# A hybrid decoder step on one core: products and weight splits moved from GpSimd to VectorE and ScalarE

## The chip, the cores and the metric

The kernel runs on one core of a Trainium2 chip. The core has a matrix engine (TensorE, PE in the profile), a vector engine (VectorE, DVE), a scalar engine (ScalarE, ACT), a general engine (GpSimd, POOL) and DMA queues, here all issued from SyncE (SP). Each engine executes its instructions in the order in which they stand in its own queue and waits on semaphores. The metric is the device time of one execution in microseconds (us), smaller being better.

## The reference

One layer of a recurrent decoder is applied to a prompt of 512 tokens and to 8 single-token samples with the same weights, all in float32. What is computed, cut to its core:

```python
xm, ig, fg, og, zm, rcols, zr, u, zs, gm = split(layer_norm(x) @ w_in)     # 1024 -> 12424 columns
# A: mLSTM: conv4, q k v, chunked exponential gating -> hm ; y_m = (hm * silu(zm)) @ w_bm
# B: RWKV-7: per token  S <- S diag(w) + (S(-kk))(kk*a)^T + v k^T ; y = S r ; y_r = (... * silu(zr)) @ w_br
# C: S5, 64 groups of 16 channels, 64 complex states each:
lb = exp(lam * dt);  bb = (lb - 1) / lam * b
s_t = lb * s_{t-1} + bb u_t ;  ys = gelu(Re(c s_t) + d u_t)
ys = ys * sigmoid(ys @ s_glu_w + s_glu_b) ;  y_s = (ys * silu(zs)) @ w_bs
x = layer_norm(ALPHA * x + (sum_b sigmoid(g_b) * y_b) @ w_out)
```

The outputs are x for prompt and samples and the new states of the three mixers.

## The kernel before

**Matrix products.** The 520 token columns stand along the free axis in two halves (256 and 264). A weight block of 1024 x 128 is loaded in two raw tiles (`load_w`, line 121, three buffers `wraw`), and each is split into a rounded high part `whi` on ScalarE (line 130) and the rest `wlo = wraw - whi` (line 131) on the engine that the list `weng` names. `gemm` then runs three products (high-high, high-low, low-high) over eight row blocks for each half and hands the PSUM tile to an evacuation on VectorE or ScalarE. `weng` is GpSimd up to the end of the RWKV stage (138 half splits) and VectorE after it (120).

**Stages.** After the entry normalisation come set-up work (the gates of the mLSTM, the S5 constants in `s5_setup`), the RWKV stage (about 100 to 745 us), the S5 stage with branch B's projections woven in (`interleave`, about 745 to 1005 us), the mLSTM stage with the S5 branch's projections woven in, and the last branch with the output product. During the RWKV stage a list of spare projections (`fills`) gives TensorE work between the recurrence's own small products.

**RWKV.** Eight channel blocks are prepared two at a time. `elementwise` builds the rows `bk` (beta rows, then scaled by the chunk's decay `pc`, and transposed to `bkt`) and `ar`. For each pair `inverse` inverts triangular blocks on VectorE: one transpose `lu`, then 31 steps of a product `itmp` and an addition `xi` (lines 589 and 591). `chain` then walks through eight chunks.

**S5.** Four passes (`pi`), each of 16 groups in two halves. A pass loads `uu` and `br` from DRAM, forms `bb` (line 959 on), then `eb` and `gm` (for each a product by `pf`'s real part on VectorE, one by its imaginary part on GpSimd, `et` and `gt`, and an addition on VectorE), and from them the kernels `ko` and, by TensorE, the drives `bu`. The phasors `ph` (64 powers of a unit complex number for 8 columns) are grown by doubling: 6 steps of 6 instructions on GpSimd, each on what the step before made. VectorE multiplies `bu` by `ph` (`ta`, `tb`, lines 1041 and 1042), scans (`z`), multiplies back (`ta` on VectorE, `tb` on GpSimd, line 1053) and writes the states `ss`, which TensorE turns into `ys`. `ph`, `bb`, `uu` have one buffer each, so that a pass's phasors begin when the pass before has last read them.

**Order.** A scheduler in the build fixes each engine's order ahead of time, so a change of engine for one instruction moves others too. Line numbers are those of the kernel before.

Of the kernel before, what the change touches and what calls it, by code (L numbers as in the profile page):

```python
# [39 lines left out]
def hybrid_step(ctx: ExitStack, tc: tile.TileContext, I, O):  # L40
    nc = tc.nc
    V, A, G, TE = nc.vector, nc.scalar, nc.gpsimd, nc.tensor
# [76 lines left out]
    weng = [G, G]  # L119
# [272 lines left out]
def rwkv(tc, I, O, env):  # L392
    e = type("E", (), env)
    nc = tc.nc
    V, A, G, TE = nc.vector, nc.scalar, nc.gpsimd, nc.tensor
# [4 lines left out]
    e.weng[:] = [G, G]  # L400
# [79 lines left out]
    def elementwise(ct, st):  # L480
        ci = ct % 2
# [28 lines left out]
        G.tensor_copy(bk[:, :, 2 * CH:3 * CH], bk[:, :, 0:CH])  # L510
# [391 lines left out]


def s5(tc, I, O, env):
# [20 lines left out]
    for pi in range(KT // 2):  # L925
# [33 lines left out]
        G.tensor_tensor(bb[:, 0], br[:, 0], cb(cr), op=ALU.mult)  # L959
        G.tensor_tensor(bt[:, 0], br[:, 1], cb(cis), op=ALU.mult)  # L960
        G.tensor_tensor(bb[:, 1], br[:, 1], cb(crs), op=ALU.mult)
        G.tensor_tensor(bt[:, 1], br[:, 0], cb(nci), op=ALU.mult)
# [11 lines left out]
        for j in range(2):  # L974
# [728 lines left out]
```

## Time and profile before

| what | value |
|---|---|
| time, median of 3 runs | 1435.56 us (1435.4 to 1437.0) |
| profiled execution, its own time | 1430.04 us |
| its span, first to last instruction | 1428.2 us |
| TensorE busy | 1291.1 us (90%) |
| VectorE busy | 952.2 us (67%) |
| ScalarE busy | 618.3 us (43%) |
| GpSimd busy | 568.4 us (40%) |
| mean granted TensorE clock | 0.954 |

Durations below come from the profiled execution. Its time is its span and 1.8 us around it, and lies 5.5 us under the median of the runs. Shares of busy time are means over stages whose limits differ, so the rows below are cut by stage.

### The profile page before, as it was taken

Reading aid. Unit: us, or ns where it says so; the run is one execution under the profiler, and the core shown is the slowest. Engines: PE = TensorE matmul, PEld = TensorE weight load, DVE = VectorE, ACT = ScalarE, POOL = GpSimd, SP = SyncE. Lnnn points to the kernel's source line nnn. Section 1 sums busy time; section 2 is a strip of 40 time slices with the busy share of each in tenths; the row PEclk is TensorE's granted clock in tenths of the full one; section 3 lists DMA queues with packets and bytes.
Section 4 is the critical chain, followed back from the end, with each engine's and each line's share of the span. In section 5 each row is a group of like instructions: output and inputs, shape, how many; then the busy total and the mean of one; then the engine's idle time right before and its main releaser. Section 6 shows DMA issues by size and latency. Waiting matters only on the chain.

```text
span 1428.2 us, 27605 instructions
## 1 busy us (share of the span) xinstructions
PE 1291.1 (90%) x10509; PEld 1162.1 (81%) x10509; DVE 952.2 (67%) x1950; ACT 618.3 (43%) x1322; POOL 568.4 (40%) x723
## 2 busy tenths in 40 slices
PE   5889989998999899998996888897899999999897
PEld 4888888877987788997976788787888798799765
DVE  6784693469336843789535997577775784665857
ACT  4446537354735463241232332232765775443230
POOL 3445544444444454447406775872000012103710
PEclk9999999999998999998998899997899999999999
DMA  5342222212221222344427453434767676466241
GB/s 181 84 117 81 80 74 63 75 42 68 66 71 42 79 64 75 96 129 149 122 69 131 105 104 91 102 77 117 225 198 255 212 224 207 149 197 194 82 118 60
DMA packets 244275, 166.92 MB, mean 117 GB/s; under 512 B 54424, under 2 KB 219674, under 8 KB 243870
## 3 DMA queue, kind: packets, MB, share of 16 engines
q1 hardware_dynamic: 244142, 165.15, 41.3%
q8 instruction: 83, 1.36, 0.4%
q14 instruction: 50, 0.41, 0.1%
HBM read 124.13 MB, written 38.68 MB: 114 GB/s over the span
## 4 chain that ended last, share of the span: by engine, by line
PE 52%; DVE 22%; POOL 8%; DMA 8%; issue 6%; ACT 3%; SPq 1%; DVEq 0%; ACTq 0%; POOLq 0%
PE g L62 33%; PE cy L62 3%; DVE xi L591 3%; DVE itmp L589 3%; PE cr L62 2%; PE gg L62 2%; POOL ph L954 1%; DVE wlo L131 1%; POOL pht L952 1%; POOL pht L953 1%; PE qk L62 1%; PE nd L62 1%; POOL et L981 1%; PE s L62 1%; PE lw L62 1%
## 5 line engine op out<-in xcount | busy, mean ns | idle before, releaser
L62 PE MATMUL g<-xh,whi 128*128 128x264 f32 (+1 forms) x1552 | 463.3, 299 | 40.2 <-DVE th L1500 15.0
L62 PE MATMUL g<-xl,whi 128*128 128x264 f32 (+1 forms) x1552 | 458.0, 295 | 1.0 <-POOL xl L217 0.5
L62 PE MATMUL g<-xh,wlo 128*128 128x264 f32 (+1 forms) x1552 | 457.2, 295 | 0.0
L62 PEld LDWEIGHTS g<-xh,whi 128*128 128x128 f32 x1552 | 303.6, 196 | 52.3 <-DVE th L1500 16.4
L62 PEld LDWEIGHTS g<-xl,whi 128*128 128x128 f32 x1552 | 303.9, 196 | 6.2 <-POOL xl L217 0.8
L62 PEld LDWEIGHTS g<-xh,wlo 128*128 128x128 f32 x1552 | 303.5, 196 | 4.9 <-issue 0.8
L130 ACT ACTIVATE whi<-wraw 128x512 fp32r<-128x512 f32 x258 | 151.6, 625 | 222.0 <-PE g L62 152.1
L131 POOL TENSOR_TENSOR wlo<-wraw,whi 128x512 fp32r<-128x512 f32 x138 | 192.7, 1416 | 134.7 <-ACT whi L130 122.6
L131 DVE TENSOR_TENSOR wlo<-wraw,whi 128x512 fp32r<-128x512 f32 x120 | 111.6, 956 | 29.5 <-ACT whi L130 27.4
L591 DVE TENSOR_TENSOR xi<-xi,itmp 128x31 f32<-128x31 f32 (+15 forms) x124 | 56.6, 456 | 3.2
L589 DVE TENSOR_TENSOR itmp<-lu,xi 128x31 f32<-128x31 f32 (+15 forms) x124 | 53.9, 435 | 3.0
L555 DVE TENSOR_TENSOR lr<-gg,maskg 64x256 f32<-64x256 f32 x32 | 13.5, 422 | 59.9 <-ACT la L554 59.8
L650 DVE SCALAR_TENSOR_TENSOR xv<-xv,pc,cy 64x64 f32<-64x64 f32 x112 | 31.2, 279 | 29.5 <-PE cy L62 24.9
L637 POOL COPY xv<-yv 64x128 f32<-64x128 f32 x64 | 24.8, 389 | 58.6 <-PE cy L62 48.2
L1547 POOL TENSOR_TENSOR mg<-mg,gth 128x256 f32<-128x256 f32 (+1 forms) x24 | 18.4, 782 | 72.6 <-DVE gth L1546 59.5
L62 PE MATMUL g<-ysh,whi 128*128 128x256 f32 (+1 forms) x128 | 38.3, 311 | 7.9 <-ACT ysh L258 5.6
L62 PE MATMUL g<-w_bmh,wlo 128*128 128x264 f32 (+1 forms) x128 | 37.5, 294 | 7.5 <-DVE wlo L131 7.4
L1547 POOL TENSOR_TENSOR mg<-mg,gt 128x256 f32<-128x256 f32 (+1 forms) x16 | 16.1, 1011 | 67.3 <-DVE gt L1546 67.3
L298 DVE COPY zf<-g 128x256 f32<-128x256 f32 (+1 forms) x56 | 23.8, 424 | 28.7 <-PE g L62 28.3
L644 DVE COPY yv<-cr 64x128 f32<-64x128 f32 x32 | 9.0, 281 | 50.2 <-PE cr L62 43.8
L1279 POOL COPY cvo<-xm 128x11 f32<-128x11 f32 x8 | 4.6, 572 | 91.9 <-ACT xm L1277 70.8
L645 ACT COPY yv<-cr 64x128 f32<-64x128 f32 x32 | 8.4, 262 | 75.6 <-DVE yv L644 75.4
(574 smaller groups left out, 3257.2 us busy)
## 6 DMA issues: line engine op xcount, KB each, us to landing
wraw<-in_w_in_dram SPq DMA_DIRECT2D x194, 256.0 KB
zsave<-zf SPq DMA_DIRECT2D x36, 260.0 KB
cn<-in_state_mlstm_c_dram SPq DMA_DIRECT2D x32, 256.0 KB
out_dram<-cn SPq DMA_DIRECT2D x32, 256.0 KB
yb<-yssave SPq DMA_DIRECT2D x16, 260.0 KB
zz<-zsave SPq DMA_DIRECT2D x16, 260.0 KB
wraw<-in_w_br_dram SPq DMA_DIRECT2D x16, 256.0 KB
wraw<-in_s_glu_w_dram SPq DMA_DIRECT2D x16, 256.0 KB
```

What stands on the lines that cost most here:

```text
L62: TE.matmul(out, lhsT, rhs, start=start, stop=stop)
L130: A.activation(hi[:, k, 0:m], raw[:, :, 0:m], AF.Copy)
L131: eng.tensor_tensor(lo[:, k, 0:m], raw[:, :, 0:m], hi[:, k, 0:m].bitcast(F32), op=ALU.subtract)
L298: V.tensor_copy(z[:, s:s + n], p)
L589: V.tensor_tensor(tv, lu[:, s + 1:32, s:s + 1].to_broadcast([P, r, w]), xi[:, s:s + 1, 0:w].to_broadcast([P, r, w]), op=ALU.mult)
L591: V.tensor_tensor(xi[:, s + 1:32, 0:w], xi[:, s + 1:32, 0:w], tv, op=ALU.add)
L637: G.tensor_copy(xv[hs(1 - pi), pi], yv[hs(1 - pi), pi, :, n, :])
L650: V.scalar_tensor_tensor(dst, xv[hs(pi), pi, ci, :], pcs[ci][hs(pi), n:n + 1], psn[hs(pi), ci, :], op0=ALU.mult, op1=ALU.add)
L952: G.tensor_tensor(tg[0], b(0), ph[:, q, :, 0:n], op=ALU.mult)
L953: G.tensor_tensor(tg[1], b(1), ph[:, 1 - q, :, 0:n], op=ALU.mult)
L954: G.tensor_tensor(ph[:, q, :, n:2 * n], tg[0], tg[1], op=ALU.add if q else ALU.subtract)
L1547: G.tensor_tensor(dst, dst, g, op=ALU.add)
```

## The change

Work is taken from GpSimd and given to VectorE and ScalarE:

- all weight splits run on VectorE (`weng` is VectorE throughout);
- the scaling of `bk` by `pc`, one GpSimd instruction of 128x1536, becomes eight ScalarE instructions of 128x192; a copy of 128x512 moves to ScalarE too;
- in S5 the products `bb`, `bt`, `et`, `gt` and `tb` run on VectorE;
- the 64 phasors are no longer grown by doubling in each pass. The set-up builds two small tables (powers 1 to 8, and multiples of 8), 40 small instructions, and writes them to DRAM in four DMAs; a pass loads its table (one DMA) and forms all 64 products with three VectorE instructions of 128x512 for each of the real and imaginary parts.

```diff
-    weng = [G, G]
+    weng = [V, V]
...
-    e.weng[:] = [G, G]
...
-        G.tensor_copy(bk[:, :, 2 * CH:3 * CH], bk[:, :, 0:CH])
+        A.activation(bk[:, :, 2 * CH:3 * CH], bk[:, :, 0:CH], AF.Copy)
...
-        G.tensor_tensor(bk, bk, st["pc"][ci].unsqueeze(2).to_broadcast([P, NCH, 3 * CH]), op=ALU.mult)
+        for n in range(NCH):
+            A.activation(bk[:, n], bk[:, n], AF.Copy, scale=st["pc"][ci][:, n:n + 1])
...
+        tb = sy.tile([P, 4, 2, 2, 8, 8], F32, name="tb")
...
+        def grow(k, by, i0, n):
+            tgs = [sy.tile([P, 4, 8, 4], F32, tag="tbt", bufs=2, name="tbt")[:, :, :, 0:n] for _ in range(2)]
+            b = lambda q: pw8(by[0], q, by[1], by[1] + 1).to_broadcast([P, 4, 8, n])
+            o = by[1] + 1
+            for q in range(2):
+                for j in range(2):
+                    V.tensor_tensor(tgs[j], b(j), pw8(k, q ^ j, i0, i0 + n), op=ALU.mult)
+                V.tensor_tensor(pw8(k, q, o, o + n), tgs[0], tgs[1], op=ALU.add if q else ALU.subtract)
...
+        for n in (1, 2, 4):
+            grow(1, (1, n - 1), 0, n)
...
+        for n in (1, 2, 4):
+            grow(0, (0, n), 1, min(n, 3))
+        for a in range(KT // 2):
+            dma(e.phsave[a], tb[:, a].rearrange("p k q c n -> p (k q c n)"))
...
-        G.tensor_copy(ph[:, :, :, 0], pr[:, 1:3, 8 * pi:8 * pi + 8])
-        n = 1
-        while n < SN:
-            b = lambda q: ph[:, q, :, n - 1:n].to_broadcast([P, 8, n])
-            for q in range(2):
-                tg = [sp.tile([P, 8, 32], F32, tag="pht", bufs=2, name="pht")[:, :, 0:n] for _ in range(2)]
-                G.tensor_tensor(tg[0], b(0), ph[:, q, :, 0:n], op=ALU.mult)
-                G.tensor_tensor(tg[1], b(1), ph[:, 1 - q, :, 0:n], op=ALU.mult)
-                G.tensor_tensor(ph[:, q, :, n:2 * n], tg[0], tg[1], op=ALU.add if q else ALU.subtract)
-            n *= 2
+        tb = sp.tile([P, 2, 2, 8, 8], F32, tag="pht", bufs=1, name="tb")
+        dma(tb.rearrange("p k q c n -> p (k q c n)"), e.phsave[pi])
+        for q in range(2):
+            tg = sp.tile([P, 8, SN], F32, tag="pg", bufs=1, name="pg")
...
+            V.tensor_tensor(v4(ph[:, q]), hi_(0), lo_(q), op=ALU.mult)
+            V.tensor_tensor(v4(tg), hi_(1), lo_(1 - q), op=ALU.mult)
+            V.tensor_tensor(ph[:, q], ph[:, q], tg, op=ALU.add if q else ALU.subtract)
...
-        G.tensor_tensor(bb, bb, bt, op=ALU.add)
+        V.tensor_tensor(bb, bb, bt, op=ALU.add)
...
-            G.tensor_tensor(et, pw(pf, 1, 0), bx(1), op=ALU.mult)
+            V.tensor_tensor(et, pw(pf, 1, 0), bx(1), op=ALU.mult)
...
-            G.tensor_tensor(gt, pw(pf, 1, 1), cx(1), op=ALU.mult)
+            V.tensor_tensor(gt, pw(pf, 1, 1), cx(1), op=ALU.mult)
...
-                G.tensor_tensor(tb, zz[1], si if q == 0 else co, op=ALU.mult)
+                V.tensor_tensor(tb, zz[1], si if q == 0 else co, op=ALU.mult)
```

What the scheduler made of it is shown at two places. The first is VectorE's queue at the first block inverse of the RWKV stage, which before holds only the inverse's own steps at its beginning:

```order
L555 TENSOR_TENSOR lr<-gg,maskg 64x256 x3
L579 STREAM_TRANSPOSE lu<-la 128x1024
L589 TENSOR_TENSOR itmp<-lu,xi 128x31
L591 TENSOR_TENSOR xi<-xi,itmp 128x31
L589 TENSOR_TENSOR itmp<-lu,xi 128x60
L591 TENSOR_TENSOR xi<-xi,itmp 128x30x2
L589 TENSOR_TENSOR itmp<-lu,xi 128x87
```

After the change the same place reads (`wlo` are weight splits of later projections; line numbers are one higher):

```order
L580 STREAM_TRANSPOSE lu<-la 128x1024
L590 TENSOR_TENSOR itmp<-lu,xi 128x31
L592 TENSOR_TENSOR xi<-xi,itmp 128x31
L590 TENSOR_TENSOR itmp<-lu,xi 128x60
L592 TENSOR_TENSOR xi<-xi,itmp 128x30x2
L590 TENSOR_TENSOR itmp<-lu,xi 128x87
L592 TENSOR_TENSOR xi<-xi,itmp 128x29x3
L131 TENSOR_TENSOR wlo<-wraw,whi 128x512
L590 TENSOR_TENSOR itmp<-lu,xi 128x112
L131 TENSOR_TENSOR wlo<-wraw,whi 128x512
L592 TENSOR_TENSOR xi<-xi,itmp 128x28x4
```

Two half splits have moved in between the inverse's steps; over the whole inverse there are 12, and 8, 8 and 12 in the other three.

The second place is GpSimd's queue in the third S5 pass before, where the phasor steps (`pht`, `ph`) and the products stand behind one another:

```order
L987 TENSOR_TENSOR gt<-pk,ca 128x1024
L981 TENSOR_TENSOR et<-pk,bb 128x1024
L954 TENSOR_TENSOR ph<-pht 128x8x4
L1048 COPY ss<-pk 128x8x8
L1049 MEMSET ss 128x8
L987 TENSOR_TENSOR gt<-pk,ca 128x1024
L959 TENSOR_TENSOR bb<-br,pk 128x256
L961 TENSOR_TENSOR bb<-br,pk 128x256
L952 TENSOR_TENSOR pht<-ph 128x8x4
L953 TENSOR_TENSOR pht<-ph 128x8x4
L963 TENSOR_TENSOR bb<-bb,bt 128x512
L954 TENSOR_TENSOR ph<-pht 128x8x4
```

After the change GpSimd holds none of these, and VectorE's queue reads, from the last states `ss` of the second pass on:

```order
L1081 TENSOR_TENSOR ss<-ta,tb 64x4x64 x4
L978 TENSOR_TENSOR ph<-tb 128x512 x2
L996 COPY ca<-ccp 128x512
L980 TENSOR_TENSOR ph<-ph,pg 128x512
L131 TENSOR_TENSOR wlo<-wraw,whi 128x512
L990 TENSOR_SCALAR cc<-cc 128x2x64
L1010 TENSOR_TENSOR gm<-pk,ca 128x1024
L1012 TENSOR_TENSOR gt<-pk,ca 128x1024
L1006 TENSOR_TENSOR et<-pk,bb 128x1024
L131 TENSOR_TENSOR wlo<-wraw,whi 128x512
L989 TENSOR_SCALAR cc<-cc 128x2x64
L979 TENSOR_TENSOR pg<-tb 128x512
```

The phasors (lines 978 to 980), `gt` and `et` (1012, 1006) now stand in VectorE's queue among its own products `gm`, `eb` and the weight splits of the branch woven in.

## Rows read from the trace of the kernel before

**Rows 1.** The page: busy us of each engine (share of the span) xinstructions.
```profile
PE 1291.1 (90%) x10509; PEld 1162.1 (81%) x10509; DVE 952.2 (67%) x1950; ACT 618.3 (43%) x1322; POOL 568.4 (40%) x723
```

**Rows 2.** Windows: three stretches; us, each engine busy (xinstructions), granted clock, DMA share, GB/s.
```profile
30.00:105.00 75.00, 64.43 (x502) 61.79 (x500) 58.99 (x154) 32.79 (x65) 33.56 (x53) 0.93 0.36 92
105.00:745.00 640.00, 606.41 (x5401) 543.73 (x5400) 389.01 (x753) 283.01 (x641) 295.62 (x354) 0.96 0.29 81
745.00:1005.00 260.00, 209.51 (x1737) 197.95 (x1736) 192.81 (x321) 81.02 (x166) 161.02 (x232) 0.90 0.48 106
```

**Rows 3.** Chain of waits from 745 to 1005 us: shares by line; one piece.
```profile
by line: issue 13.5%; POOL ph L954 8.1%; POOL pht L952 8.0%; POOL pht L953 7.7%; POOL et L981 6.7%; PE g L62 6.6%; POOL gt L987 5.5%; DVE ss L1056 3.6%; DVE z L1044 3.1%; DVE wlo L131 2.5%; DMA uu<-ud 2.4%; DMA br<-in_s_b_im_dram 2.2%; DVE 
...
760.51 5.66 DMA br<-in_s_b_im_dram
```

**Rows 4.** Timeline of GpSimd in the third S5 pass: start us, us, what.
```profile
887.95 0.35 POOL L952 TENSOR_TENSOR pht<-ph 128x8 f32<-128x8 f32 x1
...
893.84 2.05 POOL L987 TENSOR_TENSOR gt<-pk,ca 128x1024 f32<-128x1024 f32 x1
895.84 2.05 POOL L981 TENSOR_TENSOR et<-pk,bb 128x1024 f32<-128x1024 f32 x1
...
921.80 0.74 POOL L954 TENSOR_TENSOR ph<-pht 128x256 f32<-128x256 f32 x1
```

**Rows 5.** Timeline of VectorE at the same place; idle before in brackets.
```profile
920.46 0.42 DVE L1041 TENSOR_TENSOR ta<-bu,ph 128x256 f32<-128x256 f32 x1 [5.72 <-POOL ph L954]
922.57 0.42 DVE L1042 TENSOR_TENSOR tb<-bu,ph 128x256 f32<-128x256 f32 x1 [1.68 <-POOL ph L954]
```

**Rows 6.** VectorE by form, 745 to 1005 us: busy us, mean ns, idle before.
```profile
L131 DVE TENSOR_TENSOR wlo<-wraw,whi 128x512 fp32r<-128x512 f32 x42 | 35.5, 863 | 6.0 <-ACT whi L130 5.9
L988 DVE TENSOR_TENSOR gm<-gm,gt 128x1024 f32<-128x1024 f32 x8 | 16.0, 2003 | 9.4 <-POOL gt L987 9.4
...
L1594 DVE SCALAR_TENSOR_TENSOR yb<-yb,par,th 128x520 f32<-128x520 f32 x8 | 12.1, 1526 | 1.4 <-DMA yb<-ybsave 1.4
...
L1041 DVE TENSOR_TENSOR ta<-bu,ph 128x256 f32<-128x256 f32 x16 | 6.5, 408 | 16.5 <-POOL ph L954 16.4
```

**Rows 7.** Timeline, two collisions: VectorE and GpSimd each on 128x1024 products.
```profile
806.05 2.04 POOL L981 TENSOR_TENSOR et<-pk,bb 128x1024 f32<-128x1024 f32 x1
806.09 3.08 DVE L980 TENSOR_TENSOR eb<-pk,bb 128x1024 f32<-128x1024 f32 x1
...
852.32 1.24 DVE L980 TENSOR_TENSOR eb<-pk,bb 128x1024 f32<-128x1024 f32 x1
...
852.45 3.01 POOL L981 TENSOR_TENSOR et<-pk,bb 128x1024 f32<-128x1024 f32 x1
```

**Rows 8.** Line 131, the weight split: duration ns min/median/max on each engine.
```profile
L131 POOL TENSOR_TENSOR wlo<-wraw,whi x138: 1257/1290/2273, 12.3 to 707.3; 128x512 fp32r<-128x512 f32 x138
L131 DVE TENSOR_TENSOR wlo<-wraw,whi x120: 671/687/8165, 715.8 to 1352.0; 128x512 fp32r<-128x512 f32 x120
```

**Rows 9.** Windows: the four block inverses; the first and the sum.
```profile
162.70:215.10 52.40, 45.64 (x339) 43.50 (x338) 48.90 (x91) 23.17 (x48) 23.41 (x27) 0.93 0.24 66
...
sum 207.70, PE 184.23 PEld 165.44 DVE 191.89 ACT 91.27 POOL 87.03; mean PE 46.06 PEld 41.36 DVE 47.97 ACT 22.82 POOL 21.76
```

**Rows 10.** Waits of TensorE, 745 to 1005 us: total us, times, longest.
```profile
PE g L62 <- DVE th L1500: 15.0, 5, 3.6
PE ko L62 <- DVE eb L982: 8.4, 3, 3.2
```

**Rows 11.** ScalarE by line and form, 105 to 745 us.
```profile
L641 ACT ACTIVATE rs<-cr 128x128 f32<-128x128 f32 x32 | 8.9, 280 | 0.9 <-PE cr L62 0.4
...
L676 ACT ACTIVATE yr<-hm 128x256 f32<-128x256 f32 x14 | 5.3, 382 | 5.9 <-PE hm L62 5.7
```

**Rows 12.** VectorE by line and form, 69 to 89 us.
```profile
L870 DVE TENSOR_TENSOR c<-ph 128x64 f32<-128x64 f32 x3 | 0.6, 212 | 0.0
```

**Rows 13.** GpSimd by line and form, whole span.
```profile
L563 POOL TENSOR_TENSOR bk<-bk,pc 128x1536 f32<-128x1536 f32 x8 | 22.0, 2753 | 3.8 <-PE gg L62 3.8
```

More of the change, by code (lines that the diff above doesn't have):

```diff
@@ L332, in hybrid_step @@
     pksave = dr.tile([P, 2080], F32, name="pksave")
+    phsave = dr.tile([KT // 2, P, 256], F32, name="phsave")
     sh0t = fl.tile([P, 25, NB], F32, name="sh0t")
@@ L901, in s5_setup @@
         dma(e.pksave, pk)
+        tb = sy.tile([P, 4, 2, 2, 8, 8], F32, name="tb")
+        pw8 = lambda k, q, n0, n1: tb[:, :, k, q, :, n0:n1]
+        for q in range(2):
+            V.tensor_copy(pw8(1, q, 0, 1).rearrange("p a c n -> p a (c n)"), pr[:, 1 + q, :].rearrange("p (a c) -> p a c", c=8))
+            G.memset(pw8(0, q, 0, 1), 1.0 - q)
+        def grow(k, by, i0, n):
[8 more added lines that the diff above has]
+            grow(1, (1, n - 1), 0, n)
+        for q in range(2):
+            V.tensor_copy(pw8(0, q, 1, 2), pw8(1, q, 7, 8))
+        for n in (1, 2, 4):
+            grow(0, (0, n), 1, min(n, 3))
+        for a in range(KT // 2):
+            dma(e.phsave[a], tb[:, a].rearrange("p k q c n -> p (k q c n)"))
 def s5(tc, I, O, env):
@@ L945, in s5 @@
         ph = sp.tile([P, 2, 8, SN], F32, tag="ph", bufs=1, name="ph")
-        G.tensor_copy(ph[:, :, :, 0], pr[:, 1:3, 8 * pi:8 * pi + 8])
-        n = 1
-        while n < SN:
-            b = lambda q: ph[:, q, :, n - 1:n].to_broadcast([P, 8, n])
-            for q in range(2):
-                tg = [sp.tile([P, 8, 32], F32, tag="pht", bufs=2, name="pht")[:, :, 0:n] for _ in range(2)]
-                G.tensor_tensor(tg[0], b(0), ph[:, q, :, 0:n], op=ALU.mult)
-                G.tensor_tensor(tg[1], b(1), ph[:, 1 - q, :, 0:n], op=ALU.mult)
-                G.tensor_tensor(ph[:, q, :, n:2 * n], tg[0], tg[1], op=ALU.add if q else ALU.subtract)
-            n *= 2
+        tb = sp.tile([P, 2, 2, 8, 8], F32, tag="pht", bufs=1, name="tb")
+        dma(tb.rearrange("p k q c n -> p (k q c n)"), e.phsave[pi])
+        for q in range(2):
+            tg = sp.tile([P, 8, SN], F32, tag="pg", bufs=1, name="pg")
+            v4 = lambda t: t.rearrange("p c (a b) -> p c a b", b=8)
+            hi_ = lambda j: tb[:, 0, j].unsqueeze(3).to_broadcast([P, 8, 8, 8])
+            lo_ = lambda j: tb[:, 1, j].unsqueeze(2).to_broadcast([P, 8, 8, 8])
+            V.tensor_tensor(v4(ph[:, q]), hi_(0), lo_(q), op=ALU.mult)
+            V.tensor_tensor(v4(tg), hi_(1), lo_(1 - q), op=ALU.mult)
+            V.tensor_tensor(ph[:, q], ph[:, q], tg, op=ALU.add if q else ALU.subtract)
         bb = sp.tile([P, 2, 16, SC], F32, tag="bb", bufs=1, name="bb")
@@ L958, in s5 @@
         cb = lambda t: t[:, g0:g0 + 16].unsqueeze(2).to_broadcast([P, 16, SC])
[L959 to L962, printed above, removed]
-        G.tensor_tensor(bb, bb, bt, op=ALU.add)
+        V.tensor_tensor(bb[:, 0], br[:, 0], cb(cr), op=ALU.mult)
+        V.tensor_tensor(bt[:, 0], br[:, 1], cb(cis), op=ALU.mult)
+        V.tensor_tensor(bb[:, 1], br[:, 1], cb(crs), op=ALU.mult)
+        V.tensor_tensor(bt[:, 1], br[:, 0], cb(nci), op=ALU.mult)
+        V.tensor_tensor(bb, bb, bt, op=ALU.add)
         V.tensor_scalar(cc[:, :, 1, :], cc[:, :, 1, :], -1.0, None, op0=ALU.mult)
@@ L1081, in s5 @@
     tr(p[0:64, 0:P], fin)
-    fo = sp.tile([64, P], F32, tag="pht", bufs=2, name="fo")
+    fo = sp.tile([64, P], F32, tag="pht", bufs=1, name="fo")
     V.tensor_copy(fo, p[0:64, 0:P])
@@ L1090, in s5 @@
             V.tensor_copy(sb[h, q], s0[64 * q:64 * q + 64].rearrange("p b (a d) -> p b a d", d=2)[:, :, :, d])
-    t = sp.tile([P, NB, 32], F32, tag="pht", bufs=2, name="sbt")
+    t = sp.tile([P, NB, 32], F32, tag="pg", bufs=1, name="sbt")
     bcp = lambda q: pr[:, q, :].unsqueeze(1).to_broadcast([P, NB, 32])
```

## The prediction

> **What bounds the kernel now.** I read the busy times first: TensorE is busy 1291 of 1428 us, VectorE 952, GpSimd 568 [rows 1]. That makes it a TensorE kernel on average, so what moving GpSimd's work can save is found only where TensorE waits. The windows by stage say where. From 105 to 745 us (RWKV) TensorE is busy 606 of 640 us and can gain at most 34. From 745 to 1005 us (S5) it is busy 209.5 of 260 and its granted clock is the lowest of the three stretches, 0.90 of full speed against 0.93 and 0.96; some 50 us of waiting lie here [rows 2]. In the set-up (30 to 105 us) it waits 10.6 us.
>
> The chain of waits inside the S5 stage shows whom for. The phasor lines 952 to 954 on GpSimd carry 8.0 + 7.7 + 8.1 = 23.8% of it, GpSimd's products `et` and `gt` 12.2% more: 36% of 260 us, or 94 us [rows 3]. The timeline says how: in the third pass the first phasor step starts at 887.95 us and the last ends at 922.54; the 2 us products `gt` and `et` stand between the steps [rows 4]. VectorE has the drives by then but sits idle 5.72 and 1.68 us for `ph` before `ta` and `tb` [rows 5]. Over the stage VectorE idles 16.5 us before `ta` and 9.4 before `gm` for GpSimd [rows 6]. TensorE's own waits name VectorE: 15.0 us for the evacuation `th`, 8.4 for `eb` [rows 10].
>
> Second, the two engines hold each other up. At 806.05 us GpSimd starts a 128x1024 product of 2.04 us and VectorE one 0.04 us later, and VectorE's takes 3.08. At 852.32 VectorE is first and takes 1.24; GpSimd's, begun 0.13 us later, takes 3.01 [rows 7]. The later one waits for the earlier to end. So VectorE's busy time contains waiting: 42 weight splits in this stage average 863 ns [rows 6] where the median of all on VectorE is 687, with one of 8165 [rows 8].
>
> **S5 part by part.** All durations are VectorE's when alone: 1.24 us for 128x1024 [rows 7], 0.687 for 128x512 [rows 8], 0.408 for 128x256 [rows 6]. Added to VectorE over four passes: phasors 24 x 0.687 = 16.5; `bb` and `bt` 16 x 0.408 + 4 x 0.687 = 9.3; `et` and `gt` 16 x 1.24 = 19.8; `tb` 16 x 0.408 = 6.5; together 52.1 us. Given back by collisions that go: splits 42 x (863 - 687) = 7.4; `gm` 8 x (2003 - 1240) = 6.1; `yb` 8 x (1526 - 687) = 6.7 [rows 6, 8]; for the smaller two-input groups I add 8 as an estimate: 28 us. VectorE's 192.8 us become 192.8 - 28 + 52 = 217.
>
> GpSimd's 94 us leave the chain, but the stage cannot follow by that much, because VectorE's 217 us stand in one queue. It also cannot start at 745: `bb` needs `br`, which lands at 766.2 [rows 3]. Of VectorE's 67 us of idle, 26 were for GpSimd and go; 41 stay if nothing else gets better, about 20 (most of that entrance) if only the entrance stays. The stage then takes 217 + 20 = 237 to 217 + 41 = 258 us. I take 25, 242 us, nearer the low end: part of the 41 is waiting on results that collisions made late. That is **-18 us**, bounds -2 and -23. The table's load, one transfer a pass that is issued ahead of its use, costs nothing; if it came late, the pass would wait for it as it did for `ph`.
>
> **Set-up.** By its queue VectorE gets 16 splits here, 16 x 0.687 = 11.0 us, and 40 table instructions of 32 to 128 columns, priced at 0.212 us by the 128x64 product of the same set-up [rows 12]: 8.5 us. Collisions return, at the S5 stage's rate (28 of GpSimd's 161 us, 17%), 0.17 x 33.6 = 5.8. Net 13.7 us on an engine that is busy 59 of 75 [rows 2]. Bounds: nothing, if it fits the 16 idle us; 13.7, if all of it delays evacuations. I take **+4**. The four table writes stand in SP's queue ahead of weight loads and wait for the table's end; the raw tiles issued before them cover that, and without the cover it is the table's 8.5 us once more, inside the bound.
>
> **RWKV.** 118 splits come to VectorE, 118 x 0.687 = 81 us; collisions return 0.17 x 296 = 50; VectorE goes from 389 to 420 of 640 [rows 2]. For the split's consumer that is a gain: 0.69 us in the place of GpSimd's 1.29 [rows 8]. A split waiting for its high part now holds up whatever stands behind it on VectorE, evacuations above all; TensorE feels it only where VectorE has no slack, in the four inverses. There VectorE is busy 191.9 of 207.7 us and TensorE 184.2 [rows 9]. The queue puts 40 splits there, 27.5 us, against 0.17 x 87 = 15 us returned: 12.5 us into 15.8 idle ones. Bounds: +27.5 us if nothing is returned and TensorE waits for all; -8 if a third of its 23.5 us of waiting there goes. I take **0**.
>
> ScalarE's scaling: 64 instructions of 128x192, between 0.28 us (128 columns) and 0.38 (256) [rows 11], say 0.33: 2.6 us for a group in the place of one GpSimd instruction of 2.75 [rows 13]. What it gates starts no later, but ScalarE's evacuations queue behind it. ScalarE is busy 283 of 640 us [rows 2], so between 0 and 8 x 2.6 = 21 us; with the copy I take **+1**, near the low end as over half of ScalarE is idle. The entry's four splits are hidden behind TensorE's wait for the input: 0.
>
> **Sum.** -18 + 4 + 0 + 1 = -13 us: the profiled 1430.0 becomes 1417. That execution lies 5.5 us under the median of the runs, so the median becomes **1422.5**.
>
> **Rivals.** *Everything overlaps* (A): VectorE's collisions cost TensorE more than its own work does, so that TensorE bounds the S5 stage again. For it: the 15.0 us of waits for `th` alone, a short evacuation; against it: 217 us in one queue. With TensorE's waits down from 50 to 30 us and its clock from 0.90 to 0.94, the stage takes 209.5 x 0.90 / 0.94 + 30 = 231, -29; the inverses give -8, the set-up costs +2: 1430 - 35 = 1395, 1400 as a median.
>
> *VectorE is the new bound* (B): the waits of its queue stay, 41 us; S5 takes 258, -2, and the set-up and ScalarE cost +5: 1433, 1438.5, hardly a change. For it: the passes would each need 217 / 4 = 54 us of VectorE with the woven branch in it. Against it: the first pass, whose phasors can now be ready when the drives are. The Trainium skill (Perfetto Trace Analysis, section Identifying the Most-Contended Engine) says to optimise the engine with the highest occupancy first. By that rule a change that loads the 67% engine to relieve the 40% one would bring nothing, or 1438. The chain of this stage speaks against it.
>
> *The splits block the inverse* (C, slower): a split in the inverse's queue waits for its high part, the next step waits behind it, and TensorE runs out of spare projections. The price is the upper bound, +27.5 in the four windows [rows 9]: -18 + 4 + 1 + 27.5 = +14.5, 1444.5, or 1450 as a median. It decides from 13 us of those 27.5 on. Against it: 23.4 us of GpSimd's work in the first window is gone from beside the inverse.
>
> The Trainium skill (SBUF — State Buffer, section Who interferes with whom) says that a VectorE instruction with two SBUF inputs blocks only against a GpSimd instruction that reads SBUF, not against one that only writes it. What stays on GpSimd are copies and masks that do read, and fills that do not; if copies and masks still cost their full time in VectorE, less comes back than 17% says, and B gains on my forecast. Rows 7 show the block for products alone; no row here separates the two kinds.
>
> **How the numbers follow.** Forecast 47%, A 23%, B 16%, C 14%. My own case holds from 1408 to 1434, by the bounds of S5 and the set-up. To leave out no more than two in ten, the range takes in A's centre and B, and stops short of C's: 1398 to 1444. A measurement of this kernel can tell about 0.2%, 2.9 us, from no change. Faster: 44 of my own 47, all of A, 4 of B, 71%. The same: 2 + 7, 9%. Slower: 1 + 5 + 14, 20%.
>
> **What would show it.** In the changed profile: no GpSimd line in the chain of the S5 stage; `ta` of passes two to four no longer idle for `ph`; VectorE busy above 85% there; splits near 687 ns on average; the inverse windows no longer than 52.4 us and TensorE's waits in the set-up up by a few us. I am wrong if the S5 stage stays near 260 us (B), if it falls under 232 (A), or if an inverse window grows past 58 us while TensorE idles (C).

## The result and the profile after

The changed kernel takes 1394.61 us (median of four runs, 1389.74 to 1401.59) where the kernel before took 1435.48 beside it: a ratio of 0.9725, 95% interval 0.9697 to 0.9752. By the ratio that is 39.5 us, and gains below are given in the same way. The forecast was 13 us, and the time lies 3.4 us under the range of 1398 to 1444.

The page of the changed kernel, busy us of each engine, which answers to [rows 1]:

```profile
PE 1278.3 (92%) x10509; PEld 1153.7 (83%) x10509; DVE 973.1 (70%) x2204; ACT 645.9 (46%) x1394; POOL 211.0 (15%) x371
```

GpSimd lost 357 us of work; VectorE was given 254 instructions and is busy only 21 us longer. To see where the time went, I cut both executions at the same three events: the first block inverse (the first `lu`), the last state of the RWKV stage (the last `stf`), the last product of the S5 stage's outputs (the last `ys` from `ss`). Windows of the kernel before (columns as in [rows 2]):

```profile
0.00:162.70 162.70, 132.50 (x1007) 124.87 (x1008) 103.32 (x260) 83.45 (x171) 77.09 (x113) 0.96 0.41 114
162.70:739.20 576.50, 546.59 (x4949) 489.48 (x4947) 364.76 (x705) 247.09 (x559) 259.64 (x305) 0.96 0.29 80
739.20:987.70 248.50, 203.51 (x1691) 189.75 (x1691) 183.98 (x295) 78.06 (x164) 161.62 (x229) 0.91 0.47 100
987.70:1428.20 440.50, 408.53 (x2867) 357.99 (x2865) 300.10 (x691) 209.64 (x429) 70.07 (x77) 0.96 0.57 175
```

And of the changed kernel:

```profile
0.00:171.20 171.20, 140.43 (x1024) 131.75 (x1025) 112.72 (x334) 89.09 (x188) 27.86 (x77) 0.92 0.39 113
171.20:725.40 554.20, 534.89 (x4932) 481.35 (x4930) 369.08 (x810) 269.32 (x615) 98.31 (x188) 0.97 0.29 83
725.40:951.00 225.60, 200.39 (x1745) 188.63 (x1746) 196.05 (x382) 79.26 (x167) 16.91 (x31) 0.93 0.53 115
951.00:1394.20 443.20, 402.55 (x2812) 351.96 (x2810) 295.28 (x679) 208.24 (x426) 67.88 (x75) 0.95 0.57 173
```

The lengths differ by +8.5 (up to the first inverse), -22.3 (RWKV), -22.9 (S5) and +2.7 us (the rest): -34.0 between the two profiled executions. In both stages TensorE's waiting fell: from 29.9 to 19.3 us in RWKV, from 45.0 to 25.2 us in S5. The other half of RWKV's gain, 11.7 us, is TensorE's own busy time, with 17 instructions fewer in the stage and a granted clock of 0.97 in place of 0.96. The S5 stage did about what was forecast for it. The RWKV stage, forecast at 0, gave as much again.

The four inverses of the changed kernel, the first and the sum, which answer to [rows 9]:

```profile
171.20:219.90 48.70, 46.41 (x377) 44.69 (x376) 45.47 (x104) 27.39 (x58) 6.15 (x15) 1.00 0.31 84
...
sum 203.70, PE 192.85 PEld 177.08 DVE 185.72 ACT 105.85 POOL 29.84; mean PE 48.21 PEld 44.27 DVE 46.43 ACT 26.46 POOL 7.46
```

Forty half splits now stand in these windows on VectorE, 27.5 us at 0.687, and yet VectorE is busy 6.2 us less than in [rows 9]. TensorE waits 10.9 us in place of 23.5. In the first window it gets through 377 instructions where it was 339, at a granted clock of 1.00 (2.4 GHz throughout) in place of 0.93.

How the inverse's own product got shorter is seen in the listing of its line (duration ns min/median/max), before:

```profile
L589 DVE TENSOR_TENSOR itmp<-lu,xi x124: 182/380/1491, 164.8 to 619.3; 128x31 f32<-128x31 f32 x8, 128x60 f32<-128x60 f32 x8, 128x87 f32<-128x87 f32 x8, 128x112 f32<-128x112 f32 x8
```

and after:

```profile
L590 DVE TENSOR_TENSOR itmp<-lu,xi x124: 183/357/427, 173.3 to 621.0; 128x31 f32<-128x31 f32 x8, 128x60 f32<-128x60 f32 x8, 128x87 f32<-128x87 f32 x8, 128x112 f32<-128x112 f32 x8
```

Steps of up to 1491 ns are gone; none takes over 427. Over the four windows the inverse's two lines take 42.0 + 42.2 us in place of 53.9 + 56.6.

VectorE in the S5 stage, by line and form from 731 to 968 us, the same stretch after the last `stf` as the prediction's 745 to 1005, which answers to [rows 6]; and the window of that stretch, which answers to [rows 2]:

```profile
L131 DVE TENSOR_TENSOR wlo<-wraw,whi 128x512 fp32r<-128x512 f32 x42 | 27.8, 681 | 5.9 <-ACT whi L130 5.8
...
L1013 DVE TENSOR_TENSOR gm<-gm,gt 128x1024 f32<-128x1024 f32 x8 | 9.7, 1212 | 0.0
...
L1066 DVE TENSOR_TENSOR ta<-bu,ph 128x256 f32<-128x256 f32 x16 | 6.4, 401 | 0.0
```

```profile
731.00:968.00 237.00, 200.34 (x1743) 189.90 (x1742) 199.82 (x397) 80.34 (x165) 16.01 (x33) 0.91 0.55 122
```

Splits of 681 ns in place of 863, additions of 1212 in place of 2003, and `ta` no longer waits for the phasors. TensorE's wait for `th` has stayed, 15.1 us now, 7.3 of it once at the stage's entrance:

```profile
PE g L62 <- DVE th L1525: 15.1, 4, 7.3
```

### The profile page after: what moved, and what is told of

Same layout as the page of the kernel before. It is cut to its first block, busy times and chain, and to the rows that moved or that the text cites. A ratio compares the mean times of both kernels' runs of the same rounds, so it can differ in the third digit from the quotient of the medians.

```text
span 1394.2 us, 27581 instructions
## 1 busy us (share of the span) xinstructions
PE 1278.3 (92%) x10509; PEld 1153.7 (83%) x10509; DVE 973.1 (70%) x2204; ACT 645.9 (46%) x1394; POOL 211.0 (15%) x371
## 5 line engine op out<-in xcount | busy, mean ns | idle before, releaser
L62 PE MATMUL g<-xh,whi 128*128 128x256 f32 (+1 forms) x1552 | 461.6, 298 | 32.8 <-DVE th L1525 15.1
L131 DVE TENSOR_TENSOR wlo<-wraw,whi 128x512 fp32r<-128x512 f32 x258 | 194.9, 781 | 50.8 <-ACT whi L130 48.7
L62 PE MATMUL g<-ysh,whi 128*128 128x256 f32 (+1 forms) x128 | 39.2, 312 | 17.8 <-ACT ysh L258 12.5
L651 DVE SCALAR_TENSOR_TENSOR xv<-xv,pc,cy 64x64 f32<-64x64 f32 x112 | 31.2, 279 | 28.5 <-PE cy L62 25.7
L62 PE MATMUL g<-w_bmh,wlo 128*128 128x264 f32 (+1 forms) x128 | 37.2, 292 | 7.8 <-DVE wlo L131 7.8
L592 DVE TENSOR_TENSOR xi<-xi,itmp 128x31 f32<-128x31 f32 (+15 forms) x124 | 42.2, 340 | 2.8
L590 DVE TENSOR_TENSOR itmp<-lu,xi 128x31 f32<-128x31 f32 (+15 forms) x124 | 42.0, 338 | 2.6
L62 PEld LDWEIGHTS g<-ysh,whi 128*128 128x128 f32 x128 | 26.4, 210 | 19.5 <-ACT ysh L258 13.1
L62 PE MATMUL g<-ysl,whi 128*128 128x256 f32 (+1 forms) x128 | 39.2, 307 | 0.2 <-DVE ysl L260 0.2
L62 PE MATMUL g<-ysh,wlo 128*128 128x256 f32 (+1 forms) x128 | 39.0, 306 | 0.0
L62 PE MATMUL g<-bsh,whi 128*128 128x264 f32 (+1 forms) x128 | 36.9, 294 | 1.6 <-ACT bsh L258 1.6
L62 PE MATMUL g<-bsl,whi 128*128 128x264 f32 (+1 forms) x128 | 37.3, 293 | 0.0
L62 PE MATMUL g<-bsh,wlo 128*128 128x264 f32 (+1 forms) x128 | 37.2, 293 | 0.0
```

The lines of the kernel that those rows point to most:

```text
L62: TE.matmul(out, lhsT, rhs, start=start, stop=stop)
L131: eng.tensor_tensor(lo[:, k, 0:m], raw[:, :, 0:m], hi[:, k, 0:m].bitcast(F32), op=ALU.subtract)
L590: V.tensor_tensor(tv, lu[:, s + 1:32, s:s + 1].to_broadcast([P, r, w]), xi[:, s:s + 1, 0:w].to_broadcast([P, r, w]), op=ALU.mult)
L592: V.tensor_tensor(xi[:, s + 1:32, 0:w], xi[:, s + 1:32, 0:w], tv, op=ALU.add)
L651: V.scalar_tensor_tensor(dst, xv[hs(pi), pi, ci, :], pcs[ci][hs(pi), n:n + 1], psn[hs(pi), ci, :], op0=ALU.mult, op1=ALU.add)
```

## Experiments

Each run's ratio is to the kernel before on the same chip; 0.001 is 1.4 us. The lengths are those of the four stretches cut above, from each run's profile, in us. A difference between two rows is uncertain by both intervals together: from 3 us (e1 against e4) to 8 us (e6 or e7 against the changed kernel).

| kernel | ratio (95%) | to first inverse | RWKV | S5 | rest |
|---|---|---|---|---|---|
| before; again | 1 | 162.7; 165.4 | 576.5; 574.6 | 248.5; 248.2 | 440.5; 441.9 |
| changed | 0.9725 (0.9697-0.9752) | 171.2 | 554.2 | 225.6 | 443.2 |
| e1 splits back | 0.9847 (0.9832-0.9862) | 172.1 | 575.0 | 228.6 | 439.8 |
| e2 splits alone | 0.9889 (0.9874-0.9904) | 167.8 | 561.0 | 247.9 | 443.8 |
| e3 GpSimd repeats | 1.0064 (1.0044-1.0084) | 185.5 | 591.5 | 225.6 | 440.3 |
| e13 VectorE repeats | 0.9889 (0.9858-0.9920) | 176.0 | 578.2 | 225.7 | 436.2 |
| e4 S5 part alone | 0.9840 (0.9824-0.9856) | 171.5 | 577.5 | 229.9 | 434.0 |
| e5 products back | 0.9827 (0.9786-0.9867) | 169.5 | 555.5 | 230.0 | 454.6 |
| e6 phasors back | 0.9635 (0.9588-0.9682) | 166.8 | 550.5 | 226.3 | 437.5 |
| e10 tables unused | 0.9679 (0.9652-0.9707) | 169.7 | 552.3 | 220.9 | 446.5 |
| e11 products alone | 0.9843 (0.9813-0.9872) | 162.1 | 579.8 | 222.9 | 443.0 |
| e7 final on VectorE | 0.9661 (0.9613-0.9708) | 168.6 | 553.2 | 226.1 | 434.6 |
| e8 entry on GpSimd | 0.9667 (0.9631-0.9703) | 165.1 | 555.7 | 224.9 | 441.2 |
| e9 three together | 0.9631 (0.9609-0.9654) | 160.4 | 548.9 | 225.5 | 444.0 |
| e14 phasors, entry | 0.9684 (0.9645-0.9722) | 160.9 | 550.5 | 226.0 | 451.5 |
| e15 phasors, final | 0.9604 (0.9566-0.9643) | 166.3 | 548.3 | 225.5 | 430.4 |

### The splits

**e1**, the changed kernel with

```diff
-    weng = [V, V]
+    weng = [G, G]
```

> The changed kernel with the weight splits of entry, set-up and RWKV stage back on GpSimd; the S5 part and ScalarE's scaling stay. Theory 1 (the splits are what the RWKV stage gained by, about 22 us there): the RWKV stage is as long as before, the S5 stage as in the changed kernel, 1394.6 + 22 = about 1417 us (1411 to 1422), and TensorE's waiting in the four inverses is back near 23 us. Rival (the gain came from ScalarE's scaling of bk, or from the S5 part reaching back into the RWKV stage): 1395 to 1402 us.

Measured: 1414.48 us, as theory 1 says. The splits are worth 0.0122, 17.5 us, all of it and more in the RWKV stage (575.0 against 554.2). TensorE's waiting in the four inverses is 23.0 us again, as expected.

**e2**, the kernel before with

```diff
-    weng = [G, G]
+    weng = [V, V]
...
-    e.weng[:] = [G, G]
```

> The kernel before with nothing changed but the weight splits, all on VectorE. Theory 1: the RWKV stage gains its 22 us by this alone, 1435.5 - 22 = about 1413 us (1408 to 1420), TensorE's waiting in the inverses under 13 us. Rival (the gain needs GpSimd freed of the bk scaling too, whose 2.75 us instructions would collide with VectorE's): 1420 to 1430 us.

Measured: 1421.19 us, 15.9 us, on the rival's side of the line, though its RWKV stage has 15.5 of the 22 us. Some of what is missing stands ahead of the stage: the first inverse comes 5.1 us later than in the first profile of before, 2.4 later than in the second. The other 6.8 us are missing in the stage itself, and TensorE waits 14.8 us in the inverses where under 13 was expected. The rival, the scaling of `bk`, may be behind these: no run moves it alone beside moved splits.

**e3** tells collisions from the order and from the split's own speed: all queues but GpSimd's hold the changed kernel's order (two neighbouring products of TensorE apart).

```diff
-            eng.tensor_tensor(lo[:, k, 0:m], raw[:, :, 0:m], hi[:, k, 0:m].bitcast(F32), op=ALU.subtract)
+            eng.tensor_tensor(lo[:, k, 0:m], raw[:, :, 0:m], hi[:, k, 0:m].bitcast(F32), op=ALU.subtract); [G.tensor_tensor(t[:, :, 0:m], lo[:, k, 0:m].bitcast(F32), hi[:, k, 0:m].bitcast(F32), op=ALU.add) for t in dup]
```

> The changed kernel, in which GpSimd repeats an instruction of the split's kind and size (128x512, two inputs) behind every split of set-up and RWKV stage, into a tile that nobody reads. The order of TensorE, VectorE, ScalarE and the DMA queue is that of the changed kernel, word for word. Theory 1a (the gain is that of collisions: VectorE's own instructions got shorter when GpSimd's splits went): VectorE's inverse steps grow again from 21 to about 28 us an inverse, and the time goes up by 12 to 22 us, to 1407 to 1417. Rival 1b (the gain is that of the faster split, 0.69 in the place of 1.29 us, and of the spare projections that it lets TensorE's queue place earlier): no more than +3 us, 1393 to 1398.

Measured: 1445.91 us, slower than before, +0.0339 over the changed kernel or 48.7 us: theory 1a, at more than twice its price. The windows of the four inverses show the cost:

```profile
sum 234.60, PE 204.68 PEld 185.78 DVE 221.67 ACT 105.84 POOL 91.35; mean PE 51.17 PEld 46.44 DVE 55.42 ACT 26.46 POOL 22.84
```

VectorE, with the same queue, is busy 221.7 us there in place of 185.7, and the windows are 30.9 us longer; the RWKV stage as a whole loses 37.3 us. The inverse's two lines take 25.7 us an inverse in place of 21.0. Nobody reads what the 134 instructions write, and the other engines wait for them for 6.2 us in the whole run, all of it ScalarE; the rest is VectorE's lengthening and what follows from it.

**e13** gives the same repeats to VectorE (`V.tensor_tensor` in the place of `G.tensor_tensor` in the added line).

> The changed kernel in which VectorE itself does the 134 repeats that GpSimd did in the run with GpSimd's repeats (the orders of the engines differ here and there, as they hang on VectorE's load). Theory 1a (the forecast failed because it netted VectorE's own 0.69 us a split against a fixed share of GpSimd's time; beside a busy VectorE a GpSimd instruction costs more than the same instruction on VectorE itself): less than the 51 us of GpSimd's repeats, +20 to +40 us, 1415 to 1435, a ratio of 0.985 to 1.0. Rival 1c (an instruction in VectorE's queue costs at least as much as one that collides with it, so that the split's place hardly matters and the order made the gain): +50 us or more, a ratio over 1.006.

Measured: 1417.26 us, +0.0164 or 23.5 us, in theory 1a's range. An unread repeat of half a split costs the kernel 48.7 / 134 = 0.36 us on GpSimd and 0.18 on VectorE. The two are not equally sure. e3 keeps the order; in e13 TensorE's queue differs from the changed kernel's at 5829 of 10509 places, where even the kernel before differs at only 4744. So the 0.18 holds the price of another order too, and rival 1c's order can have a part in it. In the RWKV stage the two runs lie 13.3 us apart (37.3 and 24.0 us lost), less than the 20.8 us that the splits are worth there (e1): how much of the rest came by the faster split and how much by the order was not separated.

### The S5 part

**e4** is e1 with the scaling and the copy of `bk` put back on GpSimd as well.

```diff
-        for n in range(NCH):
-            A.activation(bk[:, n], bk[:, n], AF.Copy, scale=st["pc"][ci][:, n:n + 1])
+        G.tensor_tensor(bk, bk, st["pc"][ci].unsqueeze(2).to_broadcast([P, NCH, 3 * CH]), op=ALU.mult)
```

> The changed kernel with the splits back on GpSimd and the scaling and the copy of bk back too: of the change only the S5 part is left (tables, products on VectorE). If the parts add up and the S5 part is worth 18 us as forecast: 1435.5 - 18 = about 1417 us (1413 to 1424), with the S5 stage some 18 to 24 us shorter than before and the RWKV stage within 3 us of it. Rival (part of the S5 gain is that GpSimd is free for the splits that run ahead, or that the clock is higher): over 1426 us. Against the run with only the splits back it prices ScalarE's scaling: forecast +1, between 0 and 21 us in favour of this one.

Measured: 1413.41 us, 23.0 us by the S5 part with its tables; the S5 stage is 18.6 us shorter and the RWKV stage within 1.0 us, as expected. The scaling's price is the 1.0 us by which e1 is slower than e4, within the error. The parts nearly add up: 15.9 (e2) + 23.0 - 1.0 = 37.9 of the 39.5 us.

**e5**, products back on GpSimd (eight lines, of which one is shown), and **e6**, phasors grown by doubling again as in lines 946 to 955 of the kernel before, without the tables:

```diff
-            V.tensor_tensor(et, pw(pf, 1, 0), bx(1), op=ALU.mult)
+            G.tensor_tensor(et, pw(pf, 1, 0), bx(1), op=ALU.mult)
```

```diff
-        tb = sp.tile([P, 2, 2, 8, 8], F32, tag="pht", bufs=1, name="tb")
...
+        G.tensor_copy(ph[:, :, :, 0], pr[:, 1:3, 8 * pi:8 * pi + 8])
...
```

> The changed kernel with the S5 products bb, bt, et, gt and tb back on GpSimd; the phasors still come from the tables. Theory 2 (the S5 stage was bound by the phasor chain that crossed GpSimd's queue; the products' move is worth little, as VectorE loses 36 us of work and gets its collisions back): +8 us over the changed kernel, 1403 (1398 to 1409). Rival (as in the RWKV stage a GpSimd instruction beside a busy VectorE costs far more than its own time says): +15 us or more, 1410 and up.

> The changed kernel with the phasors grown by doubling on GpSimd again and without the tables of the set-up; the products stay on VectorE. Theory 2: the set-up gets back 6 to 10 us, which the runs with the S5 part on and the splits off showed as lost there, and the S5 stage loses 10 to 17 us: 1394.6 + 6 = about 1400 us (1396 to 1408). Rival (with the products gone from GpSimd's queue the doubling runs ahead by itself, and the tables bring nothing): only the set-up's gain is left, 1386 to 1391 us.

Measured: 1410.63 us with the products back, 14.6 us lost, beyond theory 2's 8 and at the rival's line (the error is 7 us). Four of them are lost in the S5 stage and 11 behind it, as TensorE gets through less of the woven branch in the stage (1596 instructions in its 230.0 us, where the changed kernel has 1745 in 225.6). Because such work moves across the stage's end, S5 and the rest are best read together: 689.0 us before, 684.6 in e5, 668.8 in the changed kernel. 1383.48 us with the phasors back: 12.9 us faster than the changed kernel, beyond even the rival. Its S5 stage is as long as with the tables, and yet the phasor lines lead its chain of waits there (the shares by line from 717.3 to 943.6 us):

```profile
by line: POOL pht L954 10.6%; POOL ph L956 10.3%; POOL pht L955 10.0%; issue 7.1%; DVE wlo L131 6.0%; DVE z L1046 4.1%; SPq L53 4.0%; DVE ss L1058 2.8%; DMA uu<-ud 2.8%; PE ys L62 2.7%; PE g L62 2.7%; DVE ta L1045 2.6%; DVE tb L1055 2.5%; D
```

The share is 30.9%, 70 us of a stage that is no shorter when the tables replace them. VectorE waits for them, in the groups by form of the same stretch, 7.3 and 4.4 us:

```profile
L1044 DVE TENSOR_TENSOR tb<-bu,ph 128x256 f32<-128x256 f32 x16 | 6.6, 415 | 4.4 <-POOL ph L956 4.4
L1043 DVE TENSOR_TENSOR ta<-bu,ph 128x256 f32<-128x256 f32 x16 | 6.5, 408 | 7.3 <-POOL ph L956 7.3
```

That is 11.7 us of waiting, which the tables take away, against the 16.5 us of work that they put on VectorE.

**e10** is e6 with the set-up's tables added again (the new lines of `s5_setup`), unread; **e11** is the kernel before with the products alone moved (the reverse of e5's edit).

> The kernel with the phasors grown on GpSimd and the products on VectorE, to which the set-up's tables (40 VectorE instructions and four writes to DRAM) are added again; nobody reads them. If the tables cost where they are built, it loses what the run without them gained in the first 180 us: +5 to +8 us over that run, a ratio to the kernel before of 0.967 to 0.969. Rival (they cost in the S5 stage, where a pass waits for its load and VectorE forms 64 phasors from them): within 2 us of the run without them, 0.963 to 0.965.

> The kernel before with nothing changed but the S5 products bb, bt, et, gt and tb, on VectorE. Theory 2a (products that stood in the phasors' way, and collided with VectorE's, were the whole of the S5 stage's loss; the phasors themselves run hidden): at least the 23 us that the whole S5 part gave, 1405 to 1413, a ratio of 0.979 to 0.984. Rival 2b, the step of the prediction (the doubling of the phasors on GpSimd bounds the stage by itself): 5 to 12 us, 0.991 to 0.997.

Measured: the unread tables cost 0.0044, 6.3 us, the size that was expected, but with an error of 8 us; the rival's 2 us are not excluded. In the profile 2.9 us are lost ahead of the first inverse; the rest comes and goes between later stages, where TensorE's order is another. The products alone give 22.5 us, the S5 part's whole gain. So far theory 2a holds, but the phasors do not run hidden, as these views of e11's S5 stage show (its window, columns as in [rows 2], and VectorE by form):

```profile
741.90:964.80 222.90, 194.57 (x1691) 182.37 (x1692) 184.14 (x346) 75.88 (x162) 104.45 (x177) 0.93 0.53 110
```

```profile
L1041 DVE TENSOR_TENSOR ta<-bu,ph 128x256 f32<-128x256 f32 x16 | 6.5, 407 | 9.3 <-POOL ph L954 9.3
```

VectorE has taken on the products, 35.6 us at the prediction's prices, and is busy 184.1 us where it was 184.0: the collisions that went paid for all of it. Its waits for GpSimd fall from 34.7 to 13.7 us. Before, they were 16.4 for `ph` ahead of `ta`, 4.5 ahead of `tb`, 9.4 for `gt`, 3.2 for `et` and 1.2 for `bb`; what is left is 9.3 and 4.4 for `ph`. So two thirds of these 21.0 us were direct waits for the products. Where the splits are on GpSimd, the tables cost nothing that shows in the time (e4 against e11), though the first inverse comes 9.4 us later with them; where VectorE has the splits too, they cost 12.9 us (changed against e6).

### Further, and both kernels beaten

**e7** moves the ten residual products of the last stage, **e8** the entry's four splits back:

```diff
-                        G.tensor_tensor(x[:n], x[:n], xg[:n, j], op=op)
+                        V.tensor_tensor(x[:n], x[:n], xg[:n, j], op=op)
```

```diff
-    weng = [V, V]
+    weng = [G, G]
...
-        ahead[C_RC + 24 * P] = load_w(I["w_in"][0, :, C_RC + 24 * P:C_RC + 24 * P + P])
+        ahead[C_RC + 24 * P] = load_w(I["w_in"][0, :, C_RC + 24 * P:C_RC + 24 * P + P]); weng[:] = [V, V]
```

> The changed kernel with GpSimd's ten residual products and additions of the last stage (eight of 128x1024, 2.6 us each) on VectorE as well. TensorE's order is the same. Theory 1a (a GpSimd instruction of that size beside VectorE's splits costs more than VectorE's own): TensorE's waits of 5.6 and 1.1 us for the last branch's splits go, VectorE gets 10 us of work and loses 22 us of collisions: -5 us, 1390 (1386 to 1393). Rival (the additions stand ahead of the splits in VectorE's queue, so that TensorE waits for them as long as it did): 1394 to 1400 us.

> The changed kernel with the four half splits of the entry alone back on GpSimd, where they were before. Theory 3 (in the changed kernel VectorE's entry splits hold up the input's preparation, TensorE waits at 16 and 23 us, and its granted clock is 0.66 from 30 to 40 us against 1.00 before): the changed kernel's loss of some 5 us in the first 50 us goes, 1390 us (1387 to 1392). Rival (the loss there is the tables' or chance): 1393 to 1397 us.

Measured: 1386.17 and 1387.20 us, both just inside the theories' ranges, gains of 9.2 and 8.3 us with errors of 8 and 6.5. For e7 the listing of line 131 in the changed kernel has a split of 8161 ns, beside these products on GpSimd:

```profile
L131 DVE TENSOR_TENSOR wlo<-wraw,whi x258: 626/684/8161, 14.3 to 1318.7; 128x512 fp32r<-128x512 f32 x129
```

In e7 the longest is 1247 ns, and the products take 1.2 us each where GpSimd needed 2.6:

```profile
L131 DVE TENSOR_TENSOR wlo<-wraw,whi x258: 626/684/1247, 15.0 to 1308.3; 128x512 fp32r<-128x512 f32 x129
```

For e8, the windows from 20 to 40 us of the changed kernel,

```profile
20.00:30.00 10.00, 7.03 (x36) 5.65 (x35) 3.46 (x9) 4.99 (x10) 1.96 (x2) 0.72 0.73 202
30.00:40.00 10.00, 8.95 (x59) 8.74 (x60) 6.29 (x24) 4.05 (x8) 3.07 (x11) 0.66 0.14 25
```

and of e8:

```profile
20.00:30.00 10.00, 7.92 (x54) 7.47 (x55) 6.21 (x20) 7.54 (x14) 2.29 (x2) 0.83 0.70 194
30.00:40.00 10.00, 10.00 (x95) 9.71 (x94) 5.49 (x18) 4.65 (x10) 2.67 (x13) 1.00 0.30 74
```

With the splits on VectorE, TensorE's waits leave it 7.03 us of work from 20 to 30 us, and its clock, at 0.72 there, is 0.66 in the next ten: much of the time at 1.2 GHz. It gets through 59 instructions in place of 95.

**e9** puts e6, e7 and e8 together; **e14** leaves e7 out of it, **e15** e8.

> The changed kernel with three of the runs above put together: the phasors grown on GpSimd without tables, the entry's four splits on GpSimd, the last stage's residual products on VectorE. If the three gains lie in different places and add up (0.9, 0.6 and 0.6 per cent), its ratio to the kernel before is 0.951, about 1366 us. Rival (the gains in the first 170 us of the runs without tables and with the entry on GpSimd are one and the same): 0.955 to 0.960, 1371 to 1378 us.

> The changed kernel with the phasors grown on GpSimd without tables and the entry's four splits on GpSimd; the last stage as in the changed kernel. In the run of three together the entry's gain of 6 us was there up to 940 us and was lost after 1000 us. If the entry's placing loses it (TensorE's order after it differs from that of the run with the phasors alone), this run is no faster than that one: 0.962 to 0.966. Rival (the last stage's additions lost it): 0.957 to 0.960.

> The changed kernel with the phasors grown on GpSimd without tables and the last stage's residual products on VectorE; the entry as in the changed kernel, TensorE's order that of the run with the phasors alone. If the last stage's gain adds to it: a ratio of 0.956 to 0.959, 1370 to 1376 us. Rival (it does not, as in the run of three together): 0.962 to 0.966.

Measured: e9 1381.96, e14 1389.22, e15 1377.11 us. None lies in a range that was expected: e9 and e14 are slower than both of their cases, though e14 is no faster than e6, as its first case says; e15, at 0.9604, falls between its two. The entry's gain is there in e9 and e14 (the first inverse 6 us earlier than in e6) and is lost in the rest (444.0 against 437.5, and 451.5): TensorE's queue has another order in e9 and e14, the same in both. What in that order costs it was not taken apart. Without that edit the last stage's gain stays (430.4 us in e15). e15 has the lowest ratio of all, 0.9604 or 57 us under the kernel before, though its interval overlaps those of e6 and e9.

**e12**, the kernel before again:

> The kernel before once more, for a second profile: its first profiled execution lay 5.5 us under the median of its runs. If that execution is a usual one, set-up, RWKV and S5 stage end within 3 us of the first profile; if not, the stage in which it was quicker shows, and the differences of stages against it are to be corrected by as much.

Measured: 1431.81 us, and its stage marks are within 3 us of the first profile's, so the differences by stage stand.

## Why the prediction was wrong, step by step

**RWKV: the step that failed.** "12.5 us into 15.8 idle ones ... I take 0". It netted 40 splits, 27.5 us, against 0.17 x 87 = 15 us returned by collisions that go. Returned were 191.9 + 27.5 - 185.7 = 33.7 us in these windows, for the 57 us of GpSimd's work that left them: 59%, not 17%. Over the whole stage it was 364.8 + 104 x 0.687 - 369.1 = 67 us for 161, or 42%.

The 17% failed because it was one price for unlike work: 28 us, in part estimated, over all that GpSimd did in the S5 stage. Measured in the same cut, this mix returned 45 of 145 us, 31%. The products alone, when they left, returned 35 of 57 us, 62% (e11). The phasor steps returned at most 12 of 86 us, 14% (e6 against the changed kernel: VectorE is busy 185.3 and 196.0 us, with 16.5 us of phasor products and some 6 us of other work that shifts in). The splits are like the products: in the windows of the inverses before, 31 of GpSimd's 32 overlap a VectorE instruction that takes over 0.15 us longer than undisturbed. That VectorE is fuller there, busy 92% of the time and not 74%, may add to it; no run separates this.

So VectorE got room and TensorE's waiting in the windows fell by 12.6 us, where the bound allowed a third of 23.5. TensorE used it for spare projections: the stretch behind the last inverse, up to the last `stf`, is 100.2 us (625.2 to 725.4) in place of 116.3 (622.9 to 739.2), with 944 instructions of TensorE in place of 1027. The stage's -22.3 us lies far outside the bounds of -8 and +27.5. e3 shows that collisions alone, at an unchanged order, are worth more than that, 37.3 us in this stage; e1 and e2 show that the gain hangs on the splits.

**S5: right in size by luck, wrong in its carrier.** Forecast -18, bounds -2 and -23; the stage gave 22.9 us in the changed kernel and 18.6 in e4. In the prediction's own cut it takes 237 us, forecast 242, but the 242 were 217 us of VectorE's work and 25 idle, and measured are 199.8 and 37.2: 45 us came back, not 28, and fewer of VectorE's waits went. The two errors nearly cancel. And "GpSimd's 94 us leave the chain" credited the phasors with 62 of them. The products alone bring the gain (e11) and the phasors' move brings nothing to the stage (e6): it takes away 11.7 us of VectorE's waits and puts 16.5 us of work in their place.

**Set-up: +4 forecast, 5.8 to 8.5 measured** against the two profiles of before, within the bound, but in good part for another reason: "hidden behind TensorE's wait for the input: 0" was wrong of the entry's four splits, which delay the first inverse by 6.1 us (e8). The tables cost 2.9 to 4.4 there (e10 and the changed kernel, each against e6), and 9.4 where the splits are on GpSimd (e4 against e11).

**Scaling: +1 forecast**, 1.0 measured (e4 against e1) where the splits are on GpSimd, within the error of 3 us; beside moved splits it was not measured (e2).

**The rivals.** A gave 1400, the nearest. Its premise, that collisions cost TensorE more than VectorE's own work does, is what e3 with e13 points to, though it placed the gain in S5 (-29) and only -8 in the inverses. B fell: in the prediction's cut the stage takes 237 us in place of 260. By the prediction's reading of the rule of the Trainium skill named there (Perfetto Trace Analysis, section Identifying the Most-Contended Engine) the time would have stayed at 1438; measured are 1394.6. C fell: the inverses' sum is 203.7 us in place of 207.7.

The signs named ahead: splits of 681 ns, `ta` without idle, and VectorE at 196 of 225.6 us (87%; 84% in the prediction's own cut) came; the longest inverse is 53.4 us, one over the mark, and TensorE's waits from 30 to 105 us are 11.4 us in place of 10.6. That no GpSimd line is left in the chain of the S5 stage could not be read, since the chain of the changed kernel does not reach back to it.

## What to carry to other kernels

Price a large two-input GpSimd instruction by the VectorE work that stands beside it: here an unread repeat of half a weight split cost the kernel 0.36 us on GpSimd, and 0.18 on VectorE in another order. Do not carry one rate from a mix: VectorE got back 62% of GpSimd's time for the large products and at most 14% for the phasor steps. A share of the chain of waits is not what its removal brings: lines with 31% of it held VectorE up for 11.7 us, and what replaced them cost as much. So ask what the replacement puts on the other engine, move the smallest piece first and look again. Gains of separate edits need not add where one edit changes an order further on.

## What was not expected of the hardware

One split of 0.68 us took 8.16 us beside GpSimd's 128x1024 products of 2.6 us, so one VectorE instruction was held up far longer than any one of them lasts. What is left on GpSimd in the inverses, copies, masks and fills (29.8 us), hardly holds VectorE up: no inverse product takes over 427 ns. In 21 places a GpSimd copy from SBUF to SBUF begins first and a step of the inverse begins before it ends; the step takes at most 19 ns longer than undisturbed, while such copies take from 190 to 1518 ns. Here it is the copy that waits. The Trainium skill (SBUF — State Buffer, section Who interferes with whom) has a VectorE instruction with two SBUF inputs contend with every GpSimd instruction that reads SBUF. The trace shows VectorE held up by large products and not by these small copies. The small phasor steps, which are products, returned little too, so size rather than kind may decide it; no run here separates the two at one size.
